# Seven feature pairs instead of four in the row-by-row end of the last product, and one lower price in the planner

## The chip, the cores and the metric

The kernel runs on one core of a Trainium2 chip. The metric is the device time of one execution in microseconds (us). Before the change three runs gave 2556.09, 2556.34 and 2561.18 us, a median of 2556.34. The profile was taken from another execution of 2554.51 us. Its span, from the first to the last instruction, is 2552.8 us, so 1.71 us lie around the span.

## The reference

One decoder layer on a sequence of 1024 tokens with 1024 features, all in float32, followed by a final normalization:

```python
x = x + 0.5 * swiglu(rmsnorm(x, ffn1_norm), ffn1_w_gate, ffn1_w_up, ffn1_w_down)
h = rmsnorm(x, mix_norm)
x = x + hybrid_mixer(h, ...)   # attention branch and gated DeltaNet branch, merged
x = x + 0.5 * swiglu(rmsnorm(x, ffn2_norm), ffn2_w_gate, ffn2_w_up, ffn2_w_down)
return rmsnorm(x, final_norm)

def swiglu(x, w_gate, w_up, w_down):
    return (silu(x @ w_gate) * (x @ w_up)) @ w_down      # 2816 hidden features
```

The DeltaNet branch has eight heads. Each needs, for every chunk of 128 tokens that the kernel works with, the inverse of a unit lower triangular 128x128 matrix.

## The kernel before, in words

**Precision.** TensorE multiplies in a reduced float32 format. Each operand is therefore split into a high part (a cast on ScalarE, `fH`) and a low part (a subtraction on VectorE, `fL`), and each product of a tile pair takes three matmuls: high by high, high by low and low by high.

**The down projections.** The class `Down` multiplies the hidden features (1024 tokens x 2816) by the down weights (2816 x 1024) with a seven-product Strassen-like scheme over halves of the tokens and of the output columns. The hidden features are kept in DRAM as the seven left combinations, each of 11 *feature pairs* of 128 rows. One product multiplies a left (128 features x 512 tokens per pair) by a right (128 features x 512 columns per pair), summed over the 11 pairs, into four PSUM banks, one for each *row block* j of 128 tokens. So a product is 11 pairs x 4 row blocks x 3 = 132 matmuls.

`Down.operands(n, p)` (line 572 before) loads left `n` of pair `p` into a tile called `hid`, casts its high part into an `fH` tile, subtracts in place so that `hid` holds the low part, and asks `right` for the two halves of the right. Every pair thus takes two `fH` tiles, one `fL` and one `hid`. The `fH` ring has 9 tiles, the `fL` ring 9; `hid` tiles come from a ring of 13 (`ff_e`, tag `e`). A tile can be filled again when its last reader is done.

`Down.product(idx, evict, outer)` runs the pairs one after the other, each through the four row blocks. The last `outer` pairs go the other way round: row block by row block, each through all of these pairs, and when a row block is complete, `evict` is called for it. Only the seventh and last product uses it, with `outer = LAST = 4`.

**The end of the program.** In the second down projection the last product's `evict` is `e4`: VectorE adds the PSUM bank to the accumulated row (`acc`, L619), ScalarE takes the square sum of the row (`sq`, L186), VectorE computes the reciprocal square root in 12 small dependent steps (L123 to L130, each on 128x1) and multiplies the row by it and by the final gain in two halves (`y`, L1493), and SyncE's queue stores each half. The rows of tokens 0 to 511 end in the product before the last, those of 512 to 1023 in the last.

**The mixer.** For each head the triangular inverse is made in 32x32 blocks on VectorE and merged on TensorE: `gdn_merge` issues 16 matmuls of 32x32 (L1074), VectorE copies the result to `W` (L1076), 16 more (L1080), VectorE copies to `Tm` (L1082) and transposes, then 8 of 64x64 (L1089), copies to `W` (L1091), and 8 more (L1096). These four groups are joined by three round trips to VectorE. TensorE fills the joints with matmuls of the input projections (L161), of the conv branch and of other heads.

**The order.** The program is built twice. After the first build, `arrange` (a list scheduler) simulates the five engines with the prices of `Program.cost` and fixes every engine's order of instructions, which the second build keeps. A price in `cost` thus changes no work, only orders. The prices of TensorE's instructions depend on their kind; kind `Q` is a matmul with at most 64 rows and columns, so the four merge groups, with `n` the number of output columns.

Of the kernel before, what the change touches and what calls it, by code (L numbers as in the profile page):

```python
# [15 lines left out]
P = 128  # L16
T = 1024
# [430 lines left out]
def ff_hidden(C, wg, wu, first, pre, begin):  # L448

    if begin:  # L450
        ff_plain(C, first, 0, 256)
    B, sums, last = ff_blocks(C)
    sums(range(3))
    a2 = []
    for f, pair in enumerate(first):
        a2 += ff_plain(C, [pair], 1, f0=f)
    a1 = [ff_e(C) for _ in range(2)]
    for n in (0, 1):
        C.nc.sync.dma_start(a1[n], C.hd[1 + n][0])
    ff_sums(C, 0, *a1, *a2)  # L460
    weights, products = ff_pair(C, wg, wu, 2, FIRST)
    weights((1, 2, 6, 3))
    products(B, FIRST[:3])
    sums((3,))
    weights((5, 7, 4))
    last()
    products(B, FIRST[3:])
    for f0 in range(4, NF, 2):
        weights, products = ff_pair(C, wg, wu, f0, STEPS)
        weights([n for n, _, _ in STEPS])  # L470
        if f0 == NF - 2:
            pre(0)
            products(B, STEPS[:1])
            pre(1)
            products(B, STEPS[1:])
        else:
            products(B, STEPS)
# [12 lines left out]
class Down:  # L490

    def __init__(self, C, wd):
        self.C = C
        self.wd = wd.rearrange("(p o k) n -> o k p n", o=2, k=P)
        self.lefts = {}
        self.raws = {}
        self.home = {}
        self.quarters = {}
        self.ops = []

    def left(self, n, p, tag="e"):
        if (n, p) not in self.lefts:
# [69 lines left out]
    def operands(self, n, p):  # L572
        C = self.C
        v = self.left(n, p)
        h = C.wp.tile([P, 512], F32R, name="fH", tag="fH", bufs=9)
        C.nc.scalar.copy(h, v.bitcast(F32))  # L576
        C.nc.vector.tensor_tensor(out=v, in0=v.bitcast(F32), in1=h.bitcast(F32), op=ALU.subtract)  # L577
        return (h, v), self.right(n, p)
# [29 lines left out]
def ff_down(C, x_dram, D_, done, mid=None):  # L608

    nc = C.nc  # L610
    acc = [None] * NT

    def part(t, n):
        if acc[t] is None:
            acc[t] = row(C, C.fx, "acc", None, None)
        return acc[t][:, n * 512:n * 512 + 512]

    def add(out, ps, base):
        nc.vector.scalar_tensor_tensor(out, ps, 0.5, base, op0=ALU.mult, op1=ALU.add)  # L619

    def e1(j, ps):
        nc.scalar.mul(part(j, 1), ps, 0.5)

    def e2(j, ps):
        add(part(j, 0), ps, part(j, 1))

    def e6(j, ps):
        add(part(j, 1), ps, part(j, 1))

    def e7(j, ps):  # L630
        add(part(4 + j, 0), ps, part(j, 1))

    def e5(j, ps):
        add(part(4 + j, 1), ps, part(4 + j, 0))
        add(part(j, 1), ps, part(j, 1))

    def residual(t):
        xt = row(C, C.fx, "xt", None, None)
        nc.sync.dma_start(xt, x_dram[t * P:t * P + P])
        nc.vector.tensor_tensor(out=acc[t], in0=acc[t], in1=xt, op=ALU.add)  # L640

    def e3(j, ps):
        add(part(j, 1), ps, part(j, 1))
        done(j, acc[j])
        acc[j] = None

    def e4(j, ps):
        add(part(4 + j, 0), ps, part(4 + j, 0))
        done(4 + j, acc[4 + j])
        acc[4 + j] = None  # L650

    def homes(p):
        if 2 <= p < 10:
            D_.load_home(p)

    def side(p):
        if p < NT:
            residual(p)
        D_.last_sums(p)

    D_.product(0, e1, side=homes)
    D_.product(1, e2)
    D_.product(2, e6)
    D_.product(3, e7)
    D_.product(4, e5)
    D_.product(5, e3, side=side)
    D_.product(6, e4, LAST, mid)


def consts(C, I):  # L670
# [761 lines left out]
def layer(tc, I, out):  # L1432
    C = Kern()
    nc = tc.nc

    def pool(name):
        return tc.tile_pool(name=name, bufs=1, reuse_waits="tile")

    with ExitStack() as st:
        open_pools(C, tc, st)  # L1440
        C.wp = st.enter_context(pool("wp"))
        ff_rings(C)
        with pool("s1") as sp:
            xs = [sp.tile([P, D], F32, name="xin", tag="xin", bufs=8) for _ in range(NT)]
            nc.sync.dma_start(xs[0], I["x"][0:P])
            gB = load_gain(C, I["ffn1_norm"])
            consts(C, I)
            for t in range(NT):
                if t:
                    nc.sync.dma_start(xs[t], I["x"][t * P:t * P + P])  # L1450
                make_h(C, xs[t], t, gB, sp, 8)()
                if t == 1:
                    W = [ff_tiles(C, I[w], 0) for w in ("ffn1_w_gate", "ffn1_w_up")]
        with pool("fx") as C.fx:
            down = Down(C, I["ffn1_w_down"])
            ff_hidden(C, I["ffn1_w_gate"], I["ffn1_w_up"], list(zip(*W)), down.start, True)
            gm = load_gain(C, I["mix_norm"])
            late = []
            first = First(C, I["w_in"])

            def done1(t, x):
                nc.sync.dma_start(C.x1d[t * P:t * P + P, :], x)
                if t % 4 == 0:
                    new_h(C, t // 4)
                late.append(make_h(C, x, t, gm, C.fx, 3))

            def mid(p):
                if p == 0:
                    first.weights()
                if p >= 3:  # L1470
                    late.pop(0)()

            ff_down(C, I["x"], down, done1, mid)
            first.blocks(range(4))
            for turn in late:
                turn()
            first.blocks(range(4, NT))
        C.fx = None
        with pool("ms") as C.ms:
            mixer(C, tc, I)  # L1480
        with pool("fx2") as C.fx:
            gB2 = load_gain(C, I["ffn2_norm"])
            first = merge_out(C, tc, I, gB2)
            down = Down(C, I["ffn2_w_down"])
            ff_hidden(C, I["ffn2_w_gate"], I["ffn2_w_up"], first, down.start, False)
            del first
            gF = load_gain(C, I["final_norm"])

            def done2(t, x):
                y = row(C, C.fx, "y", None, None)  # L1490
                r = rstd(C, x, C.fx)
                for h in (slice(0, 512), slice(512, 1024)):
                    nc.vector.scalar_tensor_tensor(y[:, h], x[:, h], r, gF[:, h], op0=ALU.mult, op1=ALU.mult)  # L1493
                    nc.sync.dma_start(out[t * P:t * P + P, h], y[:, h])

            ff_down(C, C.x2d, down, done2)
# [27 lines left out]
class Program:  # L1524
# [149 lines left out]
    def cost(self, k):  # L1674
        i = self.ins[k]
        o = i["outs"][0]
        aps = [a for a in i["ins"] if a["kind"] == "physical_ap"]
        if self.dma[k]:
            to, by = o["memref"], aps[0]["memref"]
            issue = pick(ISSUES, [to, by] if "w_down" not in by else ["fraw" if to[0] == "f" else "w_down"], 320)  # L1680
            size = 4
            for _, c in o["ap"]:
                size *= c
            run = min(2048, self.run(o), self.run(aps[0]))
            return issue, issue + 1500 + size / 434 + size / run * 0.88 + (-520 if self.place[to][0] == "DRAM" else 190)
        n = 1
        for _, c in (aps[0] if i["opcode"] == "TensorReduce" else o)["ap"][1:]:
            n *= c
        q = self.queue[k]
        if q == 0:  # L1690
            t = {"R": n / 2.4 + 13, "T": 109, "F": 223, "S": n * 0.83 + 106, "s": n * 0.83 + 106, "Q": 117 if n > 32 else 63}[self.kind[k]]
            return t, t + 190
        ps = any(self.place[a["memref"]][0] == "PSUM" for a in aps)
        if q == 1:
            t = 150 + 1.04 * n
            if len(aps) > 2:
                t += 55
            if i["opcode"] == "ISA":
                t = 82 if n == 1 else t
            elif any(a["ap"][-1][0] not in (0, 1) for a in aps) and i["opcode"] == "TensorTensor":  # L1700
                t += 0.9 * n
        elif q == 2:
            t = (160 if ps else 195) + 0.84 * n
            if len(aps) > 1:
                t += 95
            if len(i["outs"]) > 1:
                t += 90
        else:
            t = 100 + 0.9 * n + (80 if i["opcode"] == "TensorScalarAffineSelect" else 0)
        return t - (0, 82, 100, 0)[q], t  # L1710
# [175 lines left out]
```

## Time and profile before

| | |
|---|---|
| three runs | 2556.09, 2556.34, 2561.18 us |
| profiled execution | 2554.51 us, span 2552.8 us, mean granted TensorE clock 0.994 |
| TensorE matmuls busy | 2490.4 us, 98% of the span |
| VectorE busy | 1766.6 us, 69% |
| ScalarE busy | 974.1 us, 38% |
| GpSimd busy | 24.6 us, 1% |
| chain that ended last | TensorE 86%, VectorE 9%, DMA 2%, ScalarE 1%, issue 1% |

Times in a profile count from the start of the span. A row of the timeline gives start, duration, engine, line, operation, the tile written and the tiles read; in brackets stands how long the engine had been idle and what it waited for. Matmuls are pipelined: a row's duration (0.39 us for 128x512) is longer than the distance to the next one's start, which is the throughput. `L584` is the matmul of the down projections.

### The profile page before, as it was taken

Reading aid. Unit: us, or ns where it says so; the run is one execution under the profiler, and the core shown is the slowest. Engines: PE = TensorE matmul, PEld = TensorE weight load, DVE = VectorE, ACT = ScalarE, POOL = GpSimd, SP = SyncE. Lnnn points to the kernel's source line nnn. Section 1 sums busy time; section 2 is a strip of 40 time slices with the busy share of each in tenths; the row PEclk is TensorE's granted clock in tenths of the full one; section 3 lists DMA queues with packets and bytes.
Section 4 is the critical chain, followed back from the end, with each engine's and each line's share of the span. In section 5 each row is a group of like instructions: output and inputs, shape, how many; then the busy total and the mean of one; then the engine's idle time right before and its main releaser. Section 6 shows DMA issues by size and latency. Waiting matters only on the chain.

```text
span 2552.8 us, 34782 instructions
## 1 busy us (share of the span) xinstructions
PE 2490.4 (98%) x12739; PEld 2070.5 (81%) x12739; DVE 1766.6 (69%) x4035; ACT 974.1 (38%) x1875; POOL 24.6 (1%) x36
## 2 busy tenths in 40 slices
PE   7999999999999999899999999989999999999997
PEld 7888888888988888678887887868888888888886
DVE  7866666768744455988878778345768666667588
ACT  4432232444423345542444334154443332223444
POOL 0000000000000000000000000000000000000000
PEclk9999999999999999999999999999999999999999
DMA  4233224836253322322121122165542223238453
GB/s 162 84 107 119 94 101 169 288 112 219 96 138 92 92 82 80 95 57 56 55 67 53 54 57 80 55 202 189 193 138 83 92 98 120 91 118 303 137 170 119
DMA packets 257786, 301.04 MB, mean 118 GB/s; under 512 B 41456, under 2 KB 174800, under 8 KB 257616
## 3 DMA queue, kind: packets, MB, share of 16 engines
q1 hardware_dynamic: 255312, 292.53, 34.8%
q10 hardware_dynamic: 2304, 6.29, 1.1%
q8 instruction: 100, 1.64, 0.3%
q14 instruction: 70, 0.57, 0.1%
HBM read 217.34 MB, written 75.14 MB: 115 GB/s over the span
## 4 chain that ended last, share of the span: by engine, by line
PE 86%; DVE 9%; DMA 2%; ACT 1%; issue 1%; SPq 0%; DVEq 0%; ACTq 0%
PE mm L161 19%; PE tC L404 13%; PE mm L404 9%; PE tM L404 8%; PE mm L584 5%; PE tC L584 4%; PE tM L584 4%; PE tA L584 4%; PE tA L161 3%; PE mm L697 2%; PE mm L274 2%; PE tC L274 2%; PE mm L1387 2%; PE tC L1387 1%; PE tC L161 1%; PE tA L890 1%
## 5 line engine op out<-in xcount | busy, mean ns | idle before, releaser
L216 ACT CAST fH<-fraw 128x512 fp32r<-128x512 f32 x482 | 290.2, 619 | 597.8 <-PE tC L404 258.8
L217 DVE TENSOR_TENSOR fL<-fraw,fH 128x512 fp32r<-128x512 f32 x482 | 318.9, 685 | 158.9 <-ACT fH L216 142.7
L161 PE MATMUL mm<-hH,fH 128*128 128x512 f32 x896 | 359.3, 403 | 2.3 <-ACT xp L828 2.3
L161 PE MATMUL mm<-hL,fH 128*128 128x512 f32 x896 | 356.0, 398 | 0.0
L161 PE MATMUL mm<-hH,fL 128*128 128x512 f32 x896 | 353.9, 399 | 0.1
L161 PEld LDWEIGHTS mm<-hH,fH 128*128 128x128 f32 x896 | 169.1, 189 | 33.7 <-ACT xp L828 2.7
L161 PEld LDWEIGHTS mm<-hH,fL 128*128 128x128 f32 x896 | 168.9, 188 | 33.6 <-issue 1.0
L161 PEld LDWEIGHTS mm<-hL,fH 128*128 128x128 f32 x896 | 169.1, 189 | 29.9 <-issue 0.3
L404 PE MATMUL mm<-hH,fH 128*128 128x512 f32 x320 | 124.5, 389 | 0.0
L404 PE MATMUL mm<-hH,fL 128*128 128x512 f32 x320 | 123.7, 389 | 0.0
L404 PE MATMUL mm<-hL,fH 128*128 128x512 f32 x320 | 122.6, 389 | 0.0
L577 DVE TENSOR_TENSOR hid<-hid,fH 128x512 fp32r<-128x512 f32 x154 | 104.5, 684 | 9.9 <-ACT fH L576 9.9
L576 ACT CAST fH<-hid 128x512 fp32r<-128x512 f32 x154 | 94.9, 616 | 14.4 <-DMA hid<-hd1x 9.1
L969 DVE SCALAR_TENSOR_TENSOR ka<-xp,cw,ka 128x512 f32<-128x512 f32 x96 | 73.9, 781 | 19.6 <-ACT ka L967 19.0
L216 ACT CAST fH<-hH 128x512 fp32r<-128x512 f32 x68 | 42.3, 622 | 86.8 <-PE tC L584 36.0
L431 DVE TENSOR_TENSOR e<-tC,e 128x512 f32<-128x512 f32 x40 | 27.3, 686 | 66.9 <-PE tC L404 66.9
L404 PEld LDWEIGHTS mm<-hH,fL 128*128 128x128 f32 x320 | 60.1, 188 | 12.5
L404 PEld LDWEIGHTS mm<-hL,fH 128*128 128x128 f32 x320 | 60.1, 188 | 12.5
L404 PEld LDWEIGHTS mm<-hH,fH 128*128 128x128 f32 x320 | 60.1, 188 | 12.5
L584 PE MATMUL tC<-fH 128*128 128x512 f32 x176 | 68.6, 390 | 0.0
L584 PE MATMUL tC<-fL,fH 128*128 128x512 f32 x176 | 68.5, 389 | 0.0
L584 PE MATMUL mm<-fL,fH 128*128 128x512 f32 x176 | 68.4, 390 | 0.0
(402 smaller groups left out, 6111.3 us busy)
## 6 DMA issues: line engine op xcount, KB each, us to landing
fraw<-in_w_in_dram SPq DMA_DIRECT2D x66, 512.0 KB, 3.7
fraw<-in_ffn_w_gate_dram SPq DMA_DIRECT2D x22, 1024.0 KB, 5.2
fraw<-in_ffn_w_up_dram SPq DMA_DIRECT2D x22, 1024.0 KB, 7.3
hL<-in_ffn_w_down_dram SPq DMA_DIRECT2D x8, 1024.0 KB, 6.9
fraw<-in_ffn_w_down_dram SPq DMA_DIRECT2D x8, 1024.0 KB, 5.7
fraw<-in_w_branch_b_dram SPq DMA_DIRECT2D x8, 1024.0 KB, 5.1
fraw<-in_w_out_dram SPq DMA_DIRECT2D x8, 1024.0 KB, 5.3
vb<-xp ACTq DMA_DIRECT2D x48, 128.0 KB, 2.4
```

The costliest lines, as they stand in the source:

```text
L161: nc.tensor.matmul(ps, w, x, start=k == 0 and i == 0, stop=k == kt - 1 and i == 2)
L216: nc.scalar.copy(h, src)
L217: nc.vector.tensor_tensor(out=l, in0=src, in1=h.bitcast(F32), op=ALU.subtract)
L274: nc.tensor.matmul(ps[:, n0:n0 + n], w, x[:, k, c], start=k == 0 and i == 0, stop=k == KT - 1 and i == 2)
L404: nc.tensor.matmul(ps, w, x, start=opens and k == 0 and q == 0, stop=k == 3 and q == 2, skip_group_check=True)
L431: tt(out=p1[i], in0=ps, in1=p1[i], op=ALU.add)
L576: C.nc.scalar.copy(h, v.bitcast(F32))
L577: C.nc.vector.tensor_tensor(out=v, in0=v.bitcast(F32), in1=h.bitcast(F32), op=ALU.subtract)
L584: self.C.nc.tensor.matmul(ps, x[:, m], w, start=p == 0 and i == 0, stop=p == NPAIR - 1 and i == 2)
L697: nc.tensor.matmul(ps[:, :n], h[:, k, b * P:b * P + P], W[k][w], start=k == 0 and i == 0, stop=k == KT - 1 and i == 2)
L969: nc.vector.scalar_tensor_tensor(o, x, w, o, op0=ALU.mult, op1=ALU.add)
L1387: nc.tensor.matmul(ps, mx[:, c], W[k][w], start=i == 0, stop=i == len(seq) - 1)
```

## The change

There are three edits. The last product of the second down projection goes row block by row block over its last seven pairs (`closing = 7`) instead of four; the first down projection keeps four. In that product the high parts of the lefts of pairs 6 to 10 get a tile of the ring of 13 instead of an `fH` tile (`NPAIR` is 11). And the planner's price of a `Q` matmul with at most 32 columns goes from 63 to 32 ns. The code below stands four to five lines further down than before, so L584 becomes L588, L619 becomes L623, L1493 becomes L1498, and L1074, L1080, L1089, L1096 become L1078, L1084, L1093, L1100.

```diff
@@ class Down, __init__ @@
         self.ops = []
+        self.closing = 0
@@ class Down, operands @@
         v = self.left(n, p)
-        h = C.wp.tile([P, 512], F32R, name="fH", tag="fH", bufs=9)
+        if self.closing and n == 4 and p >= NPAIR - 5:
+            h = ff_e(C, "hid", F32R)
+        else:
+            h = C.wp.tile([P, 512], F32R, name="fH", tag="fH", bufs=9)
         C.nc.scalar.copy(h, v.bitcast(F32))
@@ ff_down @@
     D_.product(5, e3, side=side)
-    D_.product(6, e4, LAST, mid)
+    D_.product(6, e4, D_.closing or LAST, mid)
@@ layer @@
             down = Down(C, I["ffn2_w_down"])
+            down.closing = 7
@@ Program.cost @@
-            t = {"R": n / 2.4 + 13, "T": 109, "F": 223, "S": n * 0.83 + 106, "s": n * 0.83 + 106, "Q": 117 if n > 32 else 63}[self.kind[k]]
+            t = {"R": n / 2.4 + 13, "T": 109, "F": 223, "S": n * 0.83 + 106, "s": n * 0.83 + 106, "Q": 117 if n > 32 else 32}[self.kind[k]]
```

The orders differ in two stretches only. The price moves instructions in the mixer, from shortly before the first head's merge to the last head's; from there to the end of the second down projection's sixth product the orders are the same. The other edits move the last 170 matmuls and what belongs to them.

**TensorE, the change from the third row block to the fourth in the last product.** `tC_22433` is the bank of the third row block, `tC_22434` that of the fourth, which ends the program. `hid` names the low part of a left, after the change also the high part of the lefts of pairs 6 to 10. Before:

```order
L584 MATMUL tC_22433<-fH_22566,hid_22561 128x512
L584 MATMUL tC_22433<-fH_22587,fH_22584 128x512
L584 MATMUL tC_22433<-fL_22588,fH_22584 128x512
L584 MATMUL tC_22433<-fH_22587,hid_22582 128x512
L584 MATMUL tC_22434<-fH_22503,hid_22498 128x512
L584 MATMUL tC_22434<-fH_22524,fH_22521 128x512
```

And now:

```order
L588 MATMUL tC_22433<-fH_22551,hid_22548 128x512
L588 MATMUL tC_22433<-fL_22552,hid_22548 128x512
L588 MATMUL tC_22434<-fH_22461,fH_22458 128x512
L588 MATMUL tC_22434<-fL_22462,fH_22458 128x512
...
L588 MATMUL tC_22434<-fH_22524,hid_22521 128x512
L588 MATMUL tC_22433<-fH_22551,hid_22546 128x512
L588 MATMUL tC_22434<-fL_22525,hid_22521 128x512
```

The third row block's last matmul stood 13 matmuls ahead of the program's last one; now it stands 11 ahead, since it is placed among the fourth's. The first and second row block's last matmuls stood 33 and 26 ahead and stand 53 and 32 ahead.

**VectorE, the last row blocks.** `acc<-tC` takes a row block out of PSUM, the small steps are the reciprocal square root of the row block before. Before:

```order
3523 L619 SCALAR_TENSOR_TENSOR acc<-tC,acc 128x512
3524 L123 TENSOR_SCALAR rnv<-ssq 128x1
3525 L1493 SCALAR_TENSOR_TENSOR y<-acc,rny,gB 128x512
3526 L125 TENSOR_SCALAR rny<-rnv 128x1
3527 L126 ISA rny<-rny,magic 128x2
3528 L128 TENSOR_TENSOR rnt<-rny 128x1
3529 L129 SCALAR_TENSOR_TENSOR rnt<-rnt,rnv 128x1
3530 L130 SCALAR_TENSOR_TENSOR rny<-rnt,rny 128x1
3531 L128 TENSOR_TENSOR rnt<-rny 128x1
3532 L619 SCALAR_TENSOR_TENSOR acc<-tC,acc 128x512
```

And now:

```order
3531 L1498 SCALAR_TENSOR_TENSOR y<-acc,rny,gB 128x512
3532 L623 SCALAR_TENSOR_TENSOR acc<-tC,acc 128x512
3533 L1498 SCALAR_TENSOR_TENSOR y<-acc,rny,gB 128x512
3534 L123 TENSOR_SCALAR rnv<-ssq 128x1
3535 L125 TENSOR_SCALAR rny<-rnv 128x1
3536 L126 ISA rny<-rny,magic 128x2
3537 L623 SCALAR_TENSOR_TENSOR acc<-tC,acc 128x512
3538 L128 TENSOR_TENSOR rnt<-rny 128x1
```

Before, the fourth row block's `acc` stood in the chain of the second one, with all of the third's and the fourth's own chain behind it. Now it stands in the chain of the third, after three of its twelve steps, and only the other nine, the third's `y` and the fourth's own chain are behind it.

**TensorE, the last two joints of the first head's merge.** The L161 rows are filling work. Before:

```order
4627 L1080 MATMUL tM<-W,U 32x32 x15
4628 L161 MATMUL mm<-hH_5717,fH 128x512
4629 L161 MATMUL mm<-hL_5719,fH 128x512
4630 L161 MATMUL mm<-hH_5717,fL 128x512
4631 L161 MATMUL mm<-hH_5717,fH 128x512
4632 L161 MATMUL mm<-hL_5719,fH 128x512
4633 L1089 MATMUL tM<-Tm,ka 64x64 x8
4634 L161 MATMUL mm<-hH_5388,fH 128x512
4635 L1096 MATMUL tM<-U,W 64x64 x8
```

And now:

```order
4643 L161 MATMUL mm<-hH_5388,fL 128x512
4644 L161 MATMUL mm<-hH_5717,fL 128x512
4645 L1093 MATMUL tM<-Tm,ka 64x64 x8
4646 L161 MATMUL mm<-hH_5718,fH 128x512
4647 L161 MATMUL mm<-hL_5720,fH 128x512
4648 L161 MATMUL mm<-hH_5718,fL 128x512
4649 L161 MATMUL mm<-hH_5718,fH 128x512
4650 L161 MATMUL mm<-hL_5720,fH 128x512
4651 L161 MATMUL mm<-hH_5718,fL 128x512
4652 L161 MATMUL mm<-hH_5718,fH 128x512
4653 L161 MATMUL mm<-hL_5720,fH 128x512
4654 L1100 MATMUL tM<-U,W 64x64 x8
```

The joint ahead of the first 64x64 group had five filling matmuls and has three; the joint ahead of the second had one and has eight. The other heads move in the same manner, each by a few matmuls.

## The prediction

> **What bounds the kernel now.** I read first the busy time of each engine over the two stretches that the change touches. Columns after the length: busy us (instructions) of PE, PEld, DVE, ACT, POOL; PE's clock, DMA share, GB/s.
>
> ```profile
> 1000.00:1078.00 78.00, 70.71 (x332) 55.58 (x332) 69.37 (x244) 43.78 (x76) 2.65 (x4) 0.93 0.37 98
> 1078.00:1630.00 552.00, 539.18 (x3379) 444.08 (x3378) 434.17 (x1301) 207.26 (x402) 18.60 (x24) 1.00 0.21 59
> ...
> 2496.30:2539.40 43.10, 43.04 (x190) 35.01 (x188) 38.75 (x113) 21.90 (x39) 0.00 (x0) 1.00 0.25 87
> 2539.40:2552.80 13.40, 0.00 (x0) 0.00 (x0) 9.27 (x37) 1.15 (x2) 0.00 (x0) 0.62 0.35 135
> ```
>
> In the mixer (the first two rows) TensorE (PE) is busy 540 of 552 us and again 71 of 78: PE bounds, and what a new order can win is at most PE's waits. In the last product PE does not stand still until 2539.4; then 13.4 us follow without a matmul, in which VectorE (DVE) works 9.3 us. So the end has two bounds in turn: PE up to the last matmul, DVE behind it.
>
> Second, DVE's timeline from the first of the last four row blocks (numbered 0 to 3) on, thinned:
>
> ```profile
> 2531.85 0.69 DVE L619 SCALAR_TENSOR_TENSOR acc<-mm,acc 128x512 f32<-128x512 f32 x1 [0.84 <-PE mm L584]
> 2533.48 0.69 DVE L619 SCALAR_TENSOR_TENSOR acc<-mm,acc 128x512 f32<-128x512 f32 x1 [0.93 <-PE mm L584]
> 2534.09 0.14 DVE L123 TENSOR_SCALAR rnv<-ssq 128x1 f32<-128x1 f32 x1
> ...
> 2537.06 0.68 DVE L619 SCALAR_TENSOR_TENSOR acc<-tC,acc 128x512 f32<-128x512 f32 x1
> ...
> 2539.42 0.68 DVE L619 SCALAR_TENSOR_TENSOR acc<-tC,acc 128x512 f32<-128x512 f32 x1
> ...
> 2540.98 1.42 DVE L1493 SCALAR_TENSOR_TENSOR y<-acc,rny,gB 128x512 f32<-128x512 f32 x2
> 2542.31 0.15 DVE L123 TENSOR_SCALAR rnv<-ssq 128x1 f32<-128x1 f32 x1
> ...
> 2544.62 1.41 DVE L1493 SCALAR_TENSOR_TENSOR y<-acc,rny,gB 128x512 f32<-128x512 f32 x2
> 2545.95 0.15 DVE L123 TENSOR_SCALAR rnv<-ssq 128x1 f32<-128x1 f32 x1
> ...
> 2548.26 1.42 DVE L1493 SCALAR_TENSOR_TENSOR y<-acc,rny,gB 128x512 f32<-128x512 f32 x2
> ```
>
> One row block's ending costs DVE 0.61 us for `acc` (2533.48 to 2534.09), 2.31 for the twelve small steps (2542.31 to 2544.62, so 0.193 each) and 1.33 for `y` (2544.62 to 2545.95): 4.25 us. PE delivers row blocks faster than that:
>
> ```profile
> 2531.41 0.64 PE L584 MATMUL mm<-fH,hid 128*128 128x512 f32 x2
> ...
> 2533.05 0.39 PE L584 MATMUL mm<-fH,hid 128*128 128x512 f32 x1
> ...
> 2538.73 0.39 PE L584 MATMUL tC<-fL,fH 128*128 128x512 f32 x1
> 2538.95 0.39 PE L584 MATMUL tC<-fH,hid 128*128 128x512 f32 x1
> ```
>
> The first of the two matmuls at 2531.41 ends row block 0, the one at 2533.05 row block 1, the one at 2538.95 the program; matmuls follow each other at 0.22 to 0.23 us, I use 0.227. So the endings pile up. When row block 3 is added at 2539.42, DVE still owes the rest of row block 1, all of 2, and 3: `y` is done at 2549.68, 10.26 us later, and the span closes 3.1 us after that with the last stores.
>
> Third, PE's waits between 1000 and 1700 us, from the view of waits over the whole span (us in total, times, longest):
>
> ```profile
> PE tM L1096 <- DVE W L1091: 3.4, 6, 0.8
> PE tM L1089 <- DVE Tm L1082: 1.9, 4, 0.6
> PE tM L1080 <- DVE W L1076: 1.4, 3, 0.8
> ```
>
> These are the three joints of the heads' merges: 6.7 us of PE standing still.
>
> **The change, part by part.**
>
> *Closing.* The matmuls stay 132. The row blocks now end 53, 32, 11 and 0 matmuls before the last one. At 0.227 us that is 12.0, 7.3, 2.5 and 0 us ahead of 2538.95, that is at 2526.9, 2531.7, 2536.5 and 2538.95; their `acc` can start 0.4 us later each (2533.05 to 2533.48). The gaps between them are 4.8, 4.8 and 2.5 us against an ending of 4.25, so DVE keeps up with the first two and piles up only the last. I walk its new order with the durations above, 0.60 for a step over 512 columns and 0.07 to 0.19 for a small one, from the first ending in the product before on, where the orders are still alike:
>
> ```profile
> 2501.82 0.68 DVE L619 SCALAR_TENSOR_TENSOR acc<-tM,acc 128x512 f32<-128x512 f32 x1
> ```
>
> With the operands' subtractions in between, the chain of that product's last row block starts at about 2526.4. Row block 0's `acc` stands in it, at 2527.9; its rest and `y` take until 2530.4. Row block 0's chain ends at 2532.7, `acc` of 1 is then due, `y` until 2534.65. Row block 1's chain ends at 2537.0, its first `y` at 2537.6; `acc` of 2 starts there, 0.8 us after its bank was ready, so up to 0.8 us of lateness of PE costs nothing. The chain of 2 needs ScalarE's square sum:
>
> ```profile
> 2532.58 1.06 ACT L186 ACTIVATE sq<-acc 128x1024 f32<-128x1024 f32 x1 [2.88 <-DVE acc L619]
> 2533.55 0.18 ACT L186 ACTIVATION_READ_ACCUMULATOR sq<-acc 128x1 f32 x1
> ```
>
> From `acc` (2531.85) to the sum is 1.9 us, so the chain of 2 starts at 2539.6. Three steps, then `acc` of 3 at 2540.15, which is 0.7 us later than now. Behind it stand `acc` (0.6), nine steps (1.74), `y` of 2 (1.33), twelve steps (2.31) and `y` (1.42): 7.4 us, until 2547.6 against 2549.7. Closing: **-2.1 us**.
>
> Bounds. If nothing piled up, 3's ending alone would be 0.6, 1.3 of waiting for its square sum, 2.31 and 1.42 behind 2539.4, so 2545.0: -4.7. Above, PE's operands decide. Row block 0 now needs all 11 pairs by 2524.2 (matmul 65 before the last, 14.7 us ahead), before only by 2530. Of the nine `fH` tiles two hold the high lefts of pairs 4 and 5 and seven the rights of pairs 4 to 10, all kept until the fourth row block has read them. So the rights of 9 and 10 must wait for the tiles of pair 3, whose last matmul stands 75 before the end (2521.9, free at about 2522.3). Behind that stand a cast and a subtraction each:
>
> ```profile
> L216 ACT CAST fH<-hH 128x512 fp32r<-128x512 f32 x68 | 42.3, 622 | 86.8 <-PE tC L584 36.0
> L577 DVE TENSOR_TENSOR hid<-hid,fH 128x512 fp32r<-128x512 f32 x154 | 104.5, 684 | 9.9 <-ACT fH L576 9.9
> ```
>
> With 0.62 and 0.68 pair 9 is whole at 2523.6 to 2523.9 and is wanted at 2523.75: a wait of 0 to 0.3 us, under the 0.8 that is free. Were DVE one pair of `y` (1.33) and another subtraction late there, PE would stand some 2 us, 1.2 of them paid: closing -0.9; with a whole ending in the way (4.25), +1.6. Range -4.7 to +1.6.
>
> The tiles taken from the ring of 13 cost no time themselves; the casts are the same. The stores move ahead in the queue of SyncE by one row block, and each lands quickly:
>
> ```profile
> out_dram<-y SPq DMA_DIRECT2D x16, 256.0 KB, 2.0
> ```
>
> The 3.1 us after `y` stay.
>
> *Price.* What do 16 small matmuls take?
>
> ```profile
> 1078.49 0.69 PE L1074 MATMUL tM<-Tm,ka 32*32 32x32 f32 x32
> 1079.12 0.50 PE L161 MATMUL mm<-hH,fH 128*128 128x512 f32 x1
> ...
> 1083.21 1.41 PE L1089 MATMUL tM<-Tm,ka 64*64 64x64 f32 x16 [0.56 <-DVE Tm L1082]
> ...
> 1085.88 1.28 PE L1096 MATMUL tM<-U,W 64*64 64x64 f32 x15 [0.84 <-DVE W L1091]
> ```
>
> An instruction leaves two records here. The 32 records start within 0.69 - 0.19 = 0.50 us (0.19 is one's own length), so 31 ns per instruction: the new price is what the trace shows, the old one twice that. The plan no longer believes PE to be 0.5 us later per group than it is, and puts the groups about four matmuls later into the filling work, on average. [...]
>
> I price the new order by the joints. Ahead of L1096 the filling grows in five of eight heads (in the first from one matmul to eight) and shrinks in one that matters; six waits of 3.4/6 = 0.57 us stand there, so four net go: -2.3. Ahead of L1089 it grows in two heads that wait (4 waits of 0.48): -0.95, and shrinks by two matmuls (0.45 us) in three heads and to 0.9 us in a fourth: +1.8. Ahead of L1080 little changes. Sum **-1.4 us**.
>
> Bounds: not below -6.7 at the joints. Above, five joints have become thin (four ahead of L1089, one ahead of L1096), and DVE's queue can hold large steps ahead of a joint's copy:
>
> ```profile
> 1222.16 2.03 DVE L969 SCALAR_TENSOR_TENSOR ka<-xp,cw,ka 128x512 f32<-128x512 f32 x2
> 1224.22 0.43 DVE L1076 COPY W<-tM 32x256 f32<-32x256 f32 x1
> ```
>
> Here two steps of the convolution (2.03 us) stood ahead of it. Five times 2.03 is +10. I take -1.4, nearer to the rows of the joints themselves.
>
> *Sum.* -2.1 - 1.4 = -3.5 us. The profiled execution, 2554.51 us (span 2552.8 and 1.71 around it), would become 2551.0. The median of the runs shown lies 1.83 above that execution; against it I say 2556.34 - 3.5 = **2552.8**.
>
> **The rivals.**
>
> *Thin joints (slower).* Place: the second joint in the first, fifth, seventh and eighth head and the third in the second head. For it: these four keep only 0.7 to 0.9 us of PE work, and in the first head 1.1 us (five matmuls) already left a wait of 0.56. Against: the third joint behind three of them got fuller, so a wait in the one is partly saved in the other. It decides from 0.4 us of further wait per joint on (5 x 0.4 = the 2.1 of the closing). With 1.6 us at each it is +8, minus 2.1: +5.9, so 2562.2.
>
> *The joints empty out (faster).* The later groups find DVE ready nearly everywhere: -5 of the 6.7, and the closing gives -2.1 to -3. Sum about -7.5: 2548.8. For it: the waits at L1096 are each under 0.9 us, and the groups move by 0.9 us (four matmuls). Against: other waits come from DVE, which is busy 434 of 552 us there and stays so.
>
> *The closing gives nothing.* PE waits for the rights of pairs 9 and 10 about 2.9 us and the pile is paid for twice. For it: all nine `fH` tiles are held. Against: the free 0.8 us. With -1.4 from the mixer: 2554.9.
>
> **How the numbers follow.** The forecast, -6 to -1 us around -3.5, gets 0.52 (own range 2550.3 to 2555.3); the emptied joints 0.20; the thin joints 0.17; the closing that gives nothing 0.11. A measurement of this kernel tells a change from none at about 0.2%, 5.1 us, so faster means below 2551.2 and slower above 2561.5. Faster: 0.19 of the emptied joints and a fifth of the forecast (0.11): 0.30. Slower: 0.10, rather more than half of the thin joints. The same: 0.60. The range goes from 2547.5, which leaves out a third of the emptied joints, to 2560, which leaves out two thirds of the thin ones: below 2 in 10.
>
> **What would show it.** In the changed kernel's timeline the four `acc` at the end should lie 4.8, 4.9 and 2.5 us apart, the last 0.8 us behind the last matmul's end, and the last `y` should end 8.3 us behind that end (now 10.3); from there to the span's end 3.1 us. PE should have no wait over 0.5 us at L588 in its last 40 us. The waits at L1100 should fall from 3.4 to about 1.1 us, and those at L1093 rise from 1.9 to about 2.8; PE's idle time from 1078 to 1630 us should fall from 12.8 to about 11.4. Waits at L1093 of over 4 us, or new ones at the convolution's lines, would make the thin joints true; a wait at the first matmuls of pairs 9 or 10 of over 1 us the closing's failure. A last `y` less than 1 us sooner against the last matmul would show the walk along DVE wrong.

## The result

The changed kernel takes **2542.31 us** (median of six runs, 2538.20 to 2542.85), the kernel before 2557.38 us in the same comparison (six runs, 2556.09 to 2561.18). The ratio is 0.9937 with a 95% interval of 0.9924 to 0.9950: faster by 15 us, 13 to 19. I had said 2552.8 us, and the time lies below the range too.

The profiled execution of the changed kernel took 2542.72 us, with a span of 2541.0 us. Against the profiled one of before that is 11.8 us less. (That one was 2.9 us faster than its kernel's median, which is why the medians lie 15 apart.) The 11.8 us are in two places.

First the mixer, in the view of busy time by stretches (length, then busy us and instructions of PE, PEld, DVE, ACT, POOL; PE's granted clock, DMA share, GB/s):

```profile
1000.00:1078.00 78.00, 70.17 (x340) 55.79 (x339) 69.67 (x248) 45.48 (x77) 3.67 (x4) 0.98 0.37 99
1078.00:1630.00 552.00, 545.97 (x3417) 449.85 (x3417) 431.89 (x1305) 207.95 (x405) 19.13 (x24) 1.00 0.22 60
```

PE stands still for 7.8 us in the first row and for 6.0 us in the second, where it was 7.3 and 12.8: 6.3 us less of waiting. Counted from each head's first 32x32 group to the next head's, seven of the eight heads gave 0.6 to 1.1 us each (the eighth had no wait), and 0.5 us came on ahead of the first. The same view gives the second source, PE's granted clock, in three slices around the first head. Before:

```profile
1064.00:1068.00 4.00, 2.87 (x10) 1.94 (x10) 4.00 (x9) 2.77 (x6) 1.27 (x2) 0.59 0.01 4
1068.00:1072.00 4.00, 2.32 (x11) 1.67 (x10) 3.70 (x9) 3.99 (x8) 0.57 (x1) 0.50 0.20 33
1072.00:1076.00 4.00, 4.00 (x19) 3.58 (x19) 4.00 (x7) 2.16 (x4) 0.17 (x1) 0.63 0.60 139
```

And after:

```profile
1064.00:1068.00 4.00, 2.13 (x10) 1.21 (x10) 4.00 (x9) 3.73 (x6) 2.06 (x2) 1.00 0.02 4
1068.00:1072.00 4.00, 1.86 (x9) 1.63 (x10) 4.00 (x11) 3.92 (x8) 0.00 (x0) 0.83 0.05 8
1072.00:1076.00 4.00, 4.00 (x23) 3.57 (x23) 4.00 (x8) 1.99 (x4) 0.97 (x1) 0.74 0.54 129
```

One minus the clock, times 4 us and summed, is what the lower clock can cost at most: 5.1 us before, 1.7 after. (At 0.50 the matmuls of 128x512 started 0.43 us apart, in the changed kernel from 719.2 to 722.2 us; just behind it, at full clock, 0.23.) Less waiting and less time at half clock, together at most 6.3 + 3.4 = 9.7 us, cover the stretch: the start of PE's 9200th matmul record (1742 us before) against that of its 4800th (961 us) comes 9.8 us sooner than before.

Three of the kernels traced have PE's order of before in the mixer (before and the second and third experiment below), two the new one (the changed kernel and the first experiment). PE's idle time ahead of its records 4901 to 8900 is 20.1, 19.4 and 19.8 us in the three, 13.9 and 13.3 us in the two, so the waits belong to the order. Half clock in the same records can cost at most 5.1 us in each of the three, 1.7 and 3.4 us in the two.

Second the end. VectorE's last row blocks, and the last matmul:

```profile
2518.37 0.68 DVE L623 SCALAR_TENSOR_TENSOR acc<-mm,acc 128x512 f32<-128x512 f32 x1
2523.07 0.69 DVE L623 SCALAR_TENSOR_TENSOR acc<-mm,acc 128x512 f32<-128x512 f32 x1
...
2527.97 0.68 DVE L623 SCALAR_TENSOR_TENSOR acc<-tC,acc 128x512 f32<-128x512 f32 x1
...
2530.33 0.68 DVE L623 SCALAR_TENSOR_TENSOR acc<-tC,acc 128x512 f32<-128x512 f32 x1
2532.66 1.42 DVE L1498 SCALAR_TENSOR_TENSOR y<-acc,rny,gB 128x512 f32<-128x512 f32 x2
2536.30 1.41 DVE L1498 SCALAR_TENSOR_TENSOR y<-acc,rny,gB 128x512 f32<-128x512 f32 x2
```

```profile
2529.89 0.39 PE L588 MATMUL tC<-fH,hid 128*128 128x512 f32 x1
```

From the last matmul's start to the span's end it is 2541.0 - 2529.89 = 11.1 us, where it was 2552.8 - 2538.95 = 13.85: 2.7 us less. (Between the mixer and the end PE's work ran alike; the first 961 us came out 1.2 us later in this execution, with the same order. The last section shows where: its clock stood at 0.50 for 3.4 us at 719 us, which can cost 1.7 us, and that of before did not.)

PE's waits from 1000 to 1700 us, changed kernel (us in total, times, longest):

```profile
PE tA L983 <- ACT ka L974: 3.3, 2, 2.3
PE tM L1100 <- DVE W L1095: 1.9, 5, 0.8
PE tA L1012 <- DVE seg L999: 1.2, 2, 1.0
...
PE tM L1093 <- DVE Tm L1086: 0.5, 2, 0.3
PE tM L1084 <- DVE W L1080: 0.4, 1, 0.4
```

The three joints fell from 6.7 to 2.8 us, all three of them. The rest of the waiting that went was at other lines. (The line for `ka` at the top stood at 1.7 us in two waits before, the longest 1.3.)

### The profile page after: what moved, and what is told of

Same layout as the page of the kernel before. It is cut to its first block, busy times and chain, and to the rows that moved or that the text cites. A ratio compares the mean times of both kernels' runs of the same rounds, so it can differ in the third digit from the quotient of the medians.

```text
span 2541.0 us, 34781 instructions
## 1 busy us (share of the span) xinstructions
PE 2488.1 (98%) x12739; PEld 2069.0 (81%) x12739; DVE 1762.2 (69%) x4035; ACT 974.8 (38%) x1875; POOL 26.2 (1%) x36
## 4 chain that ended last, share of the span: by engine, by line
PE 47%; DVE 9%; DMA 1%; issue 1%; ACT 1%; SPq 0%; DVEq 0%; ACTq 0%
PE mm L161 12%; PE tC L404 6%; PE mm L404 4%; PE tM L404 4%; PE tA L161 3%; PE mm L588 2%; PE tC L588 2%; PE tM L588 2%; PE tA L588 2%; PE mm L1391 2%; PE tC L161 2%; PE tC L1391 1%; DVE fL L217 1%; DVE ka L973 1%; PE tC L274 1%
## 5 line engine op out<-in xcount | busy, mean ns | idle before, releaser
L161 PE MATMUL mm<-hH,fH 128*128 128x512 f32 x896 | 359.7, 404 | 2.2 <-ACT xp L832 2.2
L161 PE MATMUL mm<-hL,fH 128*128 128x512 f32 x896 | 357.4, 399 | 0.0
L161 PE MATMUL mm<-hH,fL 128*128 128x512 f32 x896 | 354.0, 398 | 0.0
L161 PEld LDWEIGHTS mm<-hH,fH 128*128 128x128 f32 x896 | 169.3, 189 | 34.3 <-ACT xp L832 2.6
L161 PEld LDWEIGHTS mm<-hH,fL 128*128 128x128 f32 x896 | 169.0, 189 | 33.7 <-issue 1.0
L161 PEld LDWEIGHTS mm<-hL,fH 128*128 128x128 f32 x896 | 169.4, 189 | 29.8 <-issue 0.3
L588 PE MATMUL mm<-fH,hid 128*128 128x512 f32 x186 | 70.3, 389 | 0.0
L588 PE MATMUL tC<-fH,hid 128*128 128x512 f32 x186 | 70.3, 389 | 0.0
L588 PE MATMUL tC<-fH 128*128 128x512 f32 x166 | 64.7, 390 | 0.0
```

What stands on the lines that cost most here:

```text
L161: nc.tensor.matmul(ps, w, x, start=k == 0 and i == 0, stop=k == kt - 1 and i == 2)
L588: self.C.nc.tensor.matmul(ps, x[:, m], w, start=p == 0 and i == 0, stop=p == NPAIR - 1 and i == 2)
```

## The experiments

Each comparison is with runs of the kernel before on the same chip at the same time, whose median was between 2555.1 and 2556.5 us.

### Which part gives what

The price alone, and the closing alone:

```diff
-  "Q": 117 if n > 32 else 63}          # price alone: only this
+  "Q": 117 if n > 32 else 32}
-  D_.product(6, e4, LAST, mid)         # closing alone: only these, with the tiles of the ring of 13
+  D_.product(6, e4, D_.closing or LAST, mid)
```

> The price of a Q matmul with at most 32 columns goes to 32 ns, the last product stays as before (its last four pairs row by row). The mixer's order is that of the changed kernel, so both theories of the mixer (A: the true price lets the plan put the merge groups where VectorE is ready; B: any small shift of the plan moves the time by several us either way) expect the same here: about -9 to -10 us against the kernel before, all of it between 1000 and 1750 us, with the last matmul some 9 us earlier and 13.9 us from the last matmul's start to the span's end, as before. If instead the closing moved more than the 2.7 us between the two traces (the medians of before and after differ by 15, the traces by 12), this run gives less than -9.

Measured: 2546.89 against 2556.50 us, -9.6 (ratio 0.9965, 0.9951 to 0.9978). The last matmul starts at 2531.1 us, 7.8 sooner, and 14.0 us follow it.

> Closing over seven pairs with the tiles of the ring of 13, price 63 as before. If the two parts do not touch each other: -2.7 us (the distance from the last matmul's start to the span's end falls from 13.9 to 11.1 us, PE's last matmul stays where it was). The prediction's walk along VectorE says -2.1. If the mixer's gain depended on the closing, or the closing earned more than the traces show, -5 or more.

Measured: 2552.91 against 2556.50 us, -3.6 (0.9990, 0.9981 to 0.9998). From the last matmul's start to the end 10.8 us, 3.1 less than before; PE's last matmul is where it was (2539.8). The parts add up: 9.6 + 3.6 = 13.2, just inside the interval of the whole, 13 to 19. The price gives about three quarters.

The closing without its second edit:

```diff
-        if self.closing and n == 4 and p >= NPAIR - 5:
-            h = ff_e(C, "hid", F32R)
-        else:
-            h = C.wp.tile([P, 512], F32R, name="fH", tag="fH", bufs=9)
+        h = C.wp.tile([P, 512], F32R, name="fH", tag="fH", bufs=9)
```

> Closing over seven pairs at price 63, but all high parts of the lefts stay in the ring of nine fH tiles. Seven pairs need 14 of them, so the row-by-row end cannot be held whole: in the planned order the row blocks end 35, 26, 13 and 0 matmuls before the last (before the change 33, 26, 13 and 0; with the ring of 13: 53, 32, 11 and 0). If the distance of the row blocks is what the closing gives: no change, within 1 us of the kernel before, and 13.9 us behind the last matmul's start. If the ring's tiles were beside the point, -2.7 us as with them.

Measured: 2556.70 against 2556.50 us, +0.2 (0.9994 to 1.0012), and 13.7 us behind the last matmul's start. The closing of seven gains only with the tiles: without them nothing is left. (By the planned order, the row blocks then end 35, 26, 13 and 0 matmuls before the last, nearly as before the change.)

### How much of it is the price's size

Only the number changes, with the closing as before:

```diff
-  "Q": 117 if n > 32 else 63}
+  "Q": 117 if n > 32 else 48}          # and 24, and 16
```

> The price of a Q matmul with at most 32 columns at 48 ns, half of the way, closing as before. A (an accurate price is what gains): about half of the gain, -4 to -6 us, and PE's waits at the merge's joints between those of the two kernels. B (any shift of the plan moves the time): anything between -10 and +3, with no order in the price.

> The price of a Q matmul with at most 32 columns at 24 ns, 7 under what the trace shows, old closing. If nearness to the true time is what gains (48: -4, 32: -10, 16: -5, so about 0.3 us for each ns that the price is off), -7 to -8 us. If the size at 32 was the luck of one order, as the pairs b and d (-3.5 and -3.2) suggest, -3 to -5 us like the others.

> The price of a Q matmul with at most 32 columns at 16 ns, half of what the trace shows for one (31 ns), old closing. If nearness to the true time is what gains, 16 is as far off as 47 and gives as little as 48 did: -2 to -5 us. If lower is simply better (the groups come later in the plan), -9 us or more. If the order found at 32 was a lucky one, anything, most likely -3 as with 48 and with the second neutral change.

| price, ns | 63 | 48 | 32 | 24 | 16 |
|---|---|---|---|---|---|
| median against the kernel before, us | 0 | -3.8 | -9.6 | -7.6 | -4.7 |
| PE's idle time, records 4901 to 8900, us | 20.1 | 18.0 | 13.3 | 15.3 | 17.8 |
| of it from the first 32x32 group on | 12.8 | 10.2 | 5.9 | 8.7 | 6.7 |

The gain is greatest next to the 31 ns that the trace shows for an instruction, and falls off on both sides by about 0.3 us for each ns; PE's idle time goes with it. But each price is a single order, and the re-orderings further below move the gain at 32 alone between 3 and 12 us, so the best price is not fixed to the nanosecond by this. Nor is the one side the mirror of the other. With 16 PE waits little longer from the first group on than with 32 (6.7 us for 5.9), but ahead of it a piece of the attention comes late (VectorE's `cy`, among steps of the convolution), and PE stands still once for longer than all the joints together (timeline of that kernel):

```profile
1057.70 0.66 PE L936 MATMUL tA<-ident,cy 128*128 128x128 f32 x2 [8.45 <-DVE cy L933]
```

### On which engine the price acts

The planner uses the price twice: as the time for which PE is taken, and for the moment at which VectorE may read a group's result. The two can be told different numbers:

```diff
         end = t + cost[k][1]
+        if q == 0:
+            small = small + 1 if p.kind[k] == "Q" and p.size[k] <= 32 else 0
+            end -= 31 * small      # PE 63, readers 32;   with the price at 32 and += : PE 32, readers 63
```

> The planner keeps 63 ns as the time that a Q matmul takes on PE, but tells the instructions that read a group's result the end that it would have at 32 ns; old closing. This separates the two ways in which the price acts. If the gain comes from VectorE, which plans its copies earlier and lets fewer long steps ahead of them: -7 to -10 us. If it comes from PE, whose filling work is placed by PE's own time: within 2 us of the kernel before.

Measured: 2556.91 against 2555.08 us, +1.8 (1.0013, 1.0004 to 1.0022).

> The counterpart: a Q matmul takes 32 ns on PE in the plan, but the readers of a group's result are told the end that it would have at 63 ns; old closing. If VectorE's earlier copies carry the gain: within 2 us of the kernel before. If PE's own time carries it: -7 to -10 us.

Measured: 2547.68 against 2555.08 us, -7.4 (0.9971, 0.9960 to 0.9981). So PE's own time carries most of the gain. How much the readers add is less sure than the +1.8 looks: in the trace PE's idle time in the mixer is 1.7 us less than before (18.4 for 20.1), but the mean clock of the runs is 0.9916 where that of the kernel before is 0.9933, which over the span is worth 4.1 us as an estimate (the difference times 2550 us). With PE's price alone the idle time is 15.4 us and the mean clock 0.9937. My first idea after the result had been VectorE. These are the rows between the second and the third group of the first head, before:

```profile
1080.45 0.74 DVE L969 SCALAR_TENSOR_TENSOR vT<-xp,cw,vT 128x512 f32<-128x512 f32 x1
1080.61 0.69 PE L1080 MATMUL tM<-W,U 32*32 32x32 f32 x30
1081.19 0.68 DVE L995 TENSOR_TENSOR seg<-masks,gL 128x512 fp32r<-128x512 f32 x1
...
1081.88 0.74 DVE L969 SCALAR_TENSOR_TENSOR vT<-xp,cw,vT 128x512 f32<-128x512 f32 x1
...
1082.74 0.42 DVE L1082 COPY Tm<-tM 32x256 f32<-32x256 f32 x1
...
1083.21 1.41 PE L1089 MATMUL tM<-Tm,ka 64*64 64x64 f32 x16 [0.56 <-DVE Tm L1082]
```

And after:

```profile
1083.45 0.69 PE L1084 MATMUL tM<-W,U 32*32 32x32 f32 x30
...
1084.17 0.42 DVE L1086 COPY Tm<-tM 32x256 f32<-32x256 f32 x1 [0.22 <-PE tM L1084]
...
1084.96 1.14 PE L1093 MATMUL tM<-Tm,ka 64*64 64x64 f32 x16
```

The copy starts 0.7 us behind the group's first matmul where it was 2.1, since the convolution and `seg` no longer stand ahead of it, and PE's wait is gone (no bracket). So the replies did change; but this pair of kernels says that the price told to the readers is not what pays for most of it.

The last try on VectorE's side was a rule of its own, on top of the changed kernel:

```diff
+        elif q == 1 and cost[k][0] > 500:
+            soon = [r for r, c in later[1] if r < t + cost[k][0] - 250
+                    and p.ins[c]["outs"][0]["memref"].split("_")[0] in ("W", "Tm")]
+            if soon:
+                short = [(r, c) for r, c in now[1] if not taken[c] and cost[c][0] < min(soon) - t + 100]
+                if not short:
+                    clock[1] = min(soon)
+                    continue
+                k = min(short)[1]
```

> The changed kernel (closing seven, price 32) with one rule more in the planner: VectorE does not begin a step of over 0.5 us when a copy of the merge (W or Tm) will be ready before that step would end, and takes shorter steps or stands still until then. If long steps of VectorE ahead of those copies cause what is left of PE's waits at the joints (3.4 us in the changed kernel's trace), -1 to -3 us against the changed kernel, so 2539 to 2541. If VectorE's standing still costs as much as it saves, 2542 to 2546.

Measured: 2546.11 against 2555.08 us, -9.0 (0.9965, 0.9951 to 0.9978), where the changed kernel has 0.9937 (0.9924 to 0.9950): this rule costs. Its trace has 15.2 us of waiting in the records for which the changed kernel has 13.9, and half clock that can cost 5.1 us there instead of 1.7.

### Accuracy, or one lucky order?

A list scheduler gives another order for any other number. So I gave it numbers that should be neutral, each with the price at 63 and at 32: (a) kind `F` 222 for 223; (b) VectorE's fixed price 148 for 150; (c) ScalarE's 162 and 197 for 160 and 195; (d) VectorE's 152 for 150. The closing is as before in all of them.

```diff
-  "F": 223        # a
+  "F": 222
-  t = 150 + 1.04 * n                          # b, d (VectorE)
+  t = 148 + 1.04 * n                          # d: 152
-  t = (160 if ps else 195) + 0.84 * n         # c (ScalarE)
+  t = (162 if ps else 197) + 0.84 * n
```

> A neutral change to the plan: price 63 and the old closing as before, but the price of kind F (an fp32 matmul with more than 64 columns) goes from 223 to 222 ns, so the trace gives no reason for a gain. It reorders the attention and the mixer (444 rows of PE differ, the price 32 moves 989). A (the accurate price gains): within 2 us of the kernel before. B (any shift moves the time several us): away from it by 3 us or more, either way.

> The same neutral change (kind F at 222 ns) with the Q price at 32 ns, old closing. A: -8 to -11 us against the kernel before and against the same neutral change at price 63, since the gain does not hang on one lucky order. B: the gain of the price is gone or of another size, anywhere from -10 to +3.

> A second neutral change: VectorE's fixed price per instruction goes from 150 to 148 ns, price 63, old closing. It reorders the whole program from the first feed-forward block on (1104 rows of PE differ), the mixer with it. A: mixer within 2 us of the kernel before; elsewhere a few us either way may come from the other stages, which the trace tells apart. B: the mixer (PE from 1000 to 1750 us) differs by 3 us or more.

> The second neutral change (VectorE's fixed price 148 ns) with the Q price at 32 ns, old closing. A: -8 to -11 us against the second neutral change at price 63, in the mixer. B: anywhere from -10 to +3 against it.

> A third neutral change: ScalarE's fixed price per instruction is 2 ns higher (160 and 195 become 162 and 197), price 63, old closing; 442 rows of PE in the mixer stand elsewhere. Systematic (the false price makes PE wait up to 0.5 us behind each of 16 groups, whatever else stands in the plan): within 2 us of the kernel before. Lucky order: anything from -6 to +3.

> The third neutral change with the Q price at 32 ns, old closing; 722 rows differ from the third neutral change at 63, 210 from the order with the price alone. Systematic: -6 to -11 us against the third neutral change. Lucky order: -6 to +3 against it.

> A fourth neutral change: VectorE's fixed price at 152 ns instead of 150, price 63, old closing; 848 rows of PE in the mixer stand elsewhere. Systematic: within 2 us of the kernel before, apart from what the other stages do (the trace tells them apart). Lucky order: anything from -6 to +3.

> The fourth neutral change with the Q price at 32 ns, old closing; 617 rows differ from the fourth neutral change at 63, 887 from the order with the price alone. Systematic: -6 to -11 us against the fourth neutral change. If the second neutral change was the rule and the order of the changed kernel a lucky one: -2 to -5 us.

The first three columns are medians in us. "Waits" is the sum of the idle times ahead of PE's matmul records 4901 to 8900 (from 977 to 1664 us before), in the two profiled executions. "Clock" is an estimate, the difference of the mean granted clocks of all runs of the two kernels times 2550 us; a clock of 0.001 more counts for 2.55 us.

| re-ordering | at 63 | at 32 | difference | waits | change of waits | clock |
|---|---|---|---|---|---|---|
| none | 2556.50 | 2546.89 | -9.6 | 20.1 to 13.3 | -6.8 | -2.4 |
| a | 2556.62 | 2544.66 | -12.0 | 20.0 to 14.9 | -5.1 | -3.1 |
| b | 2555.18 | 2551.73 | -3.5 | 19.7 to 17.6 | -2.0 | -0.5 |
| c | 2558.82 | 2549.18 | -9.6 | 20.7 to 15.5 | -5.2 | -2.3 |
| d | 2555.39 | 2552.19 | -3.2 | 20.1 to 15.6 | -4.5 | +3.5 |

The neutral numbers alone moved the time by -1.1 to +3.0 us against the kernel before. The price gained in every pair, and in every pair PE's waits fell; so that it gains is hardly luck. (In b and d, where it gave least, the means of the eleven runs each differ by 3.8 us, give or take 2.2 and 1.9.) How much it gains depends on the order that it meets, from 3 to 12 us, so the size of 9.6 is in part the luck of this order. Where it gave least, one pair (b) had kept more of the waits, and the other (d) lost at the clock most of what it won in waits. The change of waits and the clock together have the sign and, within 4 us, the size of the difference; what the rest of it is stays open. At the same place of PE's order in the mixer, a and c with the price have another matmul than the price alone in 440 and 404 records, b and d in 1188 and 1586, so a and c are not independent of it.

Last, neutral number a together with the whole change:

> The changed kernel with kind F at 222 ns (the first neutral change, which with price 32 and the old closing gave -12.0 against its own pair, 2.2 us lower than the price alone): if that was a real gain, 2 us below the changed kernel, about 2540; if it was noise, the same as the changed kernel within 1 us, about 2542. The closing should give its -2.7 us here as well: 2541.9 from 2544.7.

Measured: 2543.43 against 2556.13 us, -12.7 (0.9949, 0.9937 to 0.9962), with 11.1 us behind the last matmul's start. The lead of (a) did not show again: with the closing's 3.6 us its -12.0 would have become -15.6, and the -9.6 of the price alone -13.2. The intervals of this kernel and of the changed one (0.9924 to 0.9950) overlap, so these runs don't tell the two apart.

## Why the prediction was wrong

**What bounds the kernel** was right: PE in the mixer, VectorE behind the last matmul, and no matmul more or less.

**Closing** was right in mechanism and too small: -2.7 us between the traces, -3.6 by the medians, for -2.1. The four `acc` lie 4.70, 4.90 and 2.36 us apart (4.8, 4.9, 2.5 predicted), PE waited for no operand at L588, and the last `y` ends 7.4 us behind the last matmul's end (8.3 predicted, 10.3 before); the span's end follows 3.3 us later (3.1 predicted). The 0.8 us from 8.3 to 7.4 are in the start of the walk: "the chain of that product's last row block starts at about 2526.4" is 12.55 us ahead of the last matmul; it began 13.1 us ahead, and each `acc` stands 0.5 to 0.8 us earlier than walked. The bound by PE's operands did not come into play, and the third experiment shows what the second edit is for.

**Price** was the step that failed: -1.4 us for -9.6. (With other orders of the plan it would have been -3 to -12, so part of the distance is this order; but none of the five pairs gave as little as -1.4.) Three things in it were wrong.

1. "I price the new order by the joints", with the bound "not below -6.7 at the joints". The joints gave 3.9 us where 1.4 was predicted; 2.4 us of waiting net went at other lines, and up to 3.4 us of half clock. A bound on one list of waits was taken for a bound on the stretch. The row for the whole stretch, 12.8 us of PE's idle time, stood in the same prediction.
2. The term of +1.8 us ahead of L1089, for joints that become thinner. It counted PE's filling against a reply of VectorE that was taken to stay as it was. The first head's joint went from five to three filling matmuls, and its wait of 0.6 us did not grow but went, since the orders of both engines moved: VectorE's copy came 0.7 us behind the group instead of 2.1. At L1089 the waits fell from 1.9 to 0.5 us. The new order moved both engines, and the wait at a joint is the difference of the two.
3. The clock was left out. It stood at 0.59, 0.50 and 0.63 in the trace of before, in the middle of the waits that the change thins out.

What the price does, as the runs have it: at 63 ns the plan takes PE to be busy for 16 matmuls x 16 groups x 31 ns = 7.9 us longer in the mixer than it is. By that, PE comes on the chip to the next step that needs VectorE or ScalarE up to 0.5 us before the plan does, behind a group, and waits there, at a joint or further on. Told the truth, the planner puts filling work in these places. For it: most of the gain comes with PE's price alone (-7.4; readers' +1.8); of the five prices the one next to the true value gave most; and 6.3 us of waits are of the size of the 7.9.

The traces also show where the waits stood. This is PE's idle time within 5 us behind the last matmul of each of the 16 groups of 32x32:

| orders | at 63, us | at 32, us |
|---|---|---|
| before and changed | 8.5 | 1.9 |
| a | 8.1 | 1.6 |
| b | 6.2 | 2.2 |
| c | 6.6 | 1.6 |
| d | 5.0 | 5.5 |
| 32 for PE alone | | 0.8 |
| 32 for the readers alone | | 7.8 |

The first row's 6.6 us are as much as went from the mixer altogether, and the other traces with the same two orders repeat it (8.5 twice, and 1.8). The 5 us are my choice: within 4 us that row is 4.8 and 0.9, within 8 us 10.2 and 4.1. In d nothing went behind the groups, and its 4.5 us of waits went elsewhere. So in four pairs of five the waits that went stood just behind the groups; that each of them was the plan's own half microsecond is argued, not shown.

**The rivals.** The joints that empty out, at -5 of the 6.7 and 2548.8 us, came nearest; I gave it 0.20. The argument against it, that VectorE stays as busy as it was, did not hold: VectorE is still busy for 432 of 552 us, and PE waits half as long. The thin joints did not come: no wait over 0.3 us at L1093, though one of 2.3 us ahead of the first head, for the convolution's `ka` of L974 (1.3 before).

**The spacing of starts.** The 31 ns were right. In the kernel before, the 32 records of the group at 1078.5 us start in pairs: 5 to 7 ns lie within a pair and, but for the first (47 ns), 25 or 26 ns between one pair and the next. From the second pair on, one pair follows the other every 31.6 ns on average. The runs agree: a price of 48 gained 3.8 us, 32 gained 9.6 and 24 gained 7.6.

## What to carry to other kernels

Where an order comes from a planner, a first estimate of what a false price costs is what it is wrong by times how often it is used: here 31 ns, 256 times, are 8 us on the engine that bounds, and the five pairs gave 3 to 12. Bound such a change by all of the idle time of that engine in the stretch and by its clock, not by the waits at the lines that are re-priced, and take several neutral re-orderings before one order's gain is called the price's. A finer split of a last product paid here only with tiles enough to hold its operands: without the ring's tiles the same setting gave nothing.

## What the hardware showed

**Half clock came in steps, and needed no long wait.** In the mixer PE's granted clock falls to 0.50 and comes back, and what one such stretch can cost is in all 20 traces 1.7, 3.4 or 5.1 us, so 3.4 us at half clock or a multiple of it: 5.1 us around the first head before and 1.7 after, and these in two of the neutral orders at 32, first b, then d:

```profile
1148.00:1152.00 4.00, 3.45 (x19) 2.49 (x19) 3.84 (x9) 2.03 (x5) 0.00 (x0) 0.69 0.00 1
1152.00:1156.00 4.00, 4.00 (x19) 3.90 (x19) 1.92 (x7) 0.70 (x2) 0.00 (x0) 0.50 0.48 131
1156.00:1160.00 4.00, 4.00 (x25) 3.39 (x25) 3.09 (x19) 0.62 (x2) 0.00 (x0) 0.96 0.00 0
```

```profile
1380.00:1384.00 4.00, 2.24 (x29) 1.91 (x28) 3.84 (x8) 3.49 (x5) 0.00 (x0) 0.67 0.00 0
1384.00:1388.00 4.00, 4.00 (x22) 3.20 (x21) 3.91 (x8) 2.24 (x5) 0.00 (x0) 0.50 0.01 2
1388.00:1392.00 4.00, 4.00 (x22) 3.56 (x22) 3.25 (x14) 0.37 (x1) 0.00 (x0) 0.55 0.84 233
```

That is 3.4 and 5.1 us. Ahead of the one in b, which began at 1149.5 us, PE was busy for 7.97 of the 8 us from 1138 to 1146, and then had only these waits:

```profile
1146.53 0.68 PE L1093 MATMUL tM<-Tm,ka 64*64 64x64 f32 x8 [0.56 <-DVE Tm L1086]
1147.13 0.50 PE L161 MATMUL mm<-hH,fH 128*128 128x512 f32 x1
1147.47 0.60 PE L983 MATMUL tA<-ident,ka 128*128 128x128 f32 x4
1148.46 0.30 PE L1093 MATMUL tM<-Tm,ka 64*64 64x64 f32 x2 [0.39 <-DVE Tm L1086]
...
1149.35 0.95 PE L1100 MATMUL tM<-U,W 64*64 64x64 f32 x8 [0.16 <-issue]
```

No wait here was longer than 0.56 us: half clock came behind short waits among small matmuls (64x64 and 128x128). Whether the waits or the smallness of the matmuls brought it, no run here separates. In the kernel before no wait around 1064 us was longer than 1.3 us.

Nor did the length of a wait decide it. At one place ahead of the mixer, with the same order, PE waited 2.27 us in the execution of before and 2.15 us in that of the changed kernel. These are PE's row behind the wait and the view of busy time around it, before and then after:

```profile
718.27 0.50 PE L161 MATMUL mm<-hH,fH 128*128 128x512 f32 x1 [2.27 <-ACT xp L828]
716.00:724.00 8.00, 5.73 (x26) 4.77 (x26) 5.19 (x9) 3.85 (x7) 0.00 (x0) 1.00 0.46 120
```

```profile
717.87 0.50 PE L161 MATMUL mm<-hH,fH 128*128 128x512 f32 x1 [2.15 <-ACT xp L832]
716.00:724.00 8.00, 6.13 (x20) 4.87 (x21) 5.54 (x11) 3.86 (x7) 0.00 (x0) 0.79 0.39 101
```

The longer wait was followed by the full clock, the shorter by 3.4 us at 0.50.

**The spread between runs of one kernel went with the clock.** Of 27 runs of the kernel before (those of the first experiments), the ten at a mean clock of 0.993 took 2555.8 us on average, the seven at 0.992 took 2558.2, and the eight at 0.994 took 2554.6. The steps, 2.4 and 1.2 us, are of the order of the 2.55 us that 0.001 of the span stands for. So two profiled executions with the same order need not agree to better than a few us.
